# A two-layer hybrid decoder on one Trainium2 core: the first mixer's key selection placed later in the engines' order

## The chip, the cores and the metric

The kernel runs on one core of one Trainium2 chip. The metric is the device time of one execution in microseconds (us), lower is better. The engines are named as in the profile: PE is TensorE (matmuls), PEld its weight loads, DVE VectorE, ACT ScalarE, POOL GpSimd, SP the sync engine, whose queue issues nearly all transfers. A row with a q (SPq) is an engine's own queue of transfers.

## The reference

Two decoder layers over 512 positions of width 1024, all in float32. Both layers are feed-forward, mixer, feed-forward; the first layer's mixer is the one that the change is about. Cut to what matters there:

```python
for layer in range(2):
    h = h + 0.5 * swiglu(rmsnorm(h, g[0]), ...)      # 1024 -> 2816 -> 1024
    h = h + (hybrid_ab_mixer if layer == 0 else swa_sink_mixer)(rmsnorm(h, g[1]), ...)
    h = h + 0.5 * swiglu(rmsnorm(h, g[2]), ...)

def hybrid_ab_mixer(u, table, w_in, cq_g, wq_b, wq_idx, w_out):
    qa, ka, va, cq, kb, vb, k_idx, w_idx = split(u @ w_in)
    o_a = dilated_mixture(qa, ka, va, table[:, :8])          # heads 0 to 7, no selection
    cq = rmsnorm(cq, cq_g)
    qb, q_idx = cq @ wq_b, cq @ wq_idx                       # q_idx: 8 index heads of 32
    # selection: score[t, s] = scale * sum_h w_idx[t, h] * relu(q_idx[t, h] . k_idx[s]), s <= t
    # each position keeps its 128 best keys (topk = min(256, 512 // 4))
    o_b = dsa_attention(qb, kb, vb, q_idx, k_idx, w_idx, table[:, 8:], 128)   # heads 8 to 15
    return concatenate([o_a, o_b]) @ w_out
```

Every head adds a relative-position bias, whose table (32 buckets by 16 heads) is shared by all. Only heads 8 to 15 of the first mixer read the selection.

## The kernel before, in words

Activations lie transposed in SBUF, eight tiles of 128 features by 512 positions. Products are made in three matmuls on operands that are split into a high part (a cast) and a low part (a subtraction): high by low, low by high, high by high. These are L366 to L368 for the projections, L581 to L583 in the feed-forward, L748 and L749 for a head's logits. So each weight that comes in (L328, 512 KB) is cast on ScalarE (L336) and subtracted from by the helper `sub` (L315), on VectorE or, where the call allows it, on GpSimd. Keys and queries of a head pair are split the same way (casts L372, copies L693/L696, low parts L315).

**Who sets the order.** The kernel first describes every operation (`Plan.op`): the engines that may run it, a model duration, what it reads and writes, and a number `v`, its place in a nominal TensorE time `vt` that grows by each matmul's model duration. Then `Plan.emit` makes the order, one operation at a time: of each engine's candidates whose inputs are planned it takes the one that its model lets start first, and among those within 20 ns the one of smallest `v`. Buffers are slots of fixed pools (58 of 128x512 called s2, 20 weight tiles called d4, 8 PSUM banks), with limits per kind (`LIMIT`, `RESERVE`); `slot_time` answers whether and when an operation's buffers are to be had. An engine then runs its instructions in exactly that order, so an instruction that waits holds up all behind it, on SP's queue too.

**The first mixer** (`hybrid`). First come two products for the low-rank query, the index keys `kst` and the eight query stacks `qst`, each put together by three transfers from SBUF to SBUF (L891, 24 in all, on SP). Then `project(0)` makes value, key and query of the first two heads. `select` lists the selection: 24 scores, for three blocks of 128 queries times eight index heads, each a matmul (L932, 256, 384 or 512 columns) into a PSUM bank of which it may have four, a relu on ScalarE (L935) and a weighted sum on VectorE (L939, L942 for the first of a block, L946 for the others); then 16 rounds of MAX8 (L954) and MATCH_REPLACE8 (L956) for each block on VectorE, each taking the eight largest out; then three masks (L962). It gives these steps values `v` spread evenly between two numbers. After it come, for j from 0 to 7, `attend(j)` (two heads) and `project(j + 1)`; only j of 4 and more reads the masks.

**The bias tables.** GpSimd's queue writes the 16 tables of the first mixer (`tab0`) and those of the last (`tab1`) to memory in the first part of the run. Each head loads its own (L661, by SP) into an s2 slot of the kind `toep`, of which there may be five at a time; a load's `v` is 8000 below the nominal time at which it is described.

The constants are `SELECT_NS = 135000` and those quoted with the change. Line numbers are those of the profile before; in the changed kernel the same lines stand 2 to 7 further down (L366 is L373, L336 is L343, L315 is L322, L328 is L335, L372 is L379, L661 is L668, L748 is L755, L932 is L939, L935 is L942).

Of the kernel before, what the change touches and what calls it, by code (L numbers as in the profile page):

```python
# [35 lines left out]

LIMIT = {'mm': 4, 'sc': 2, 'sci': 4, 'pt': 2, 'ptv': 1, 'o': 6, 'tmp': 6, 'relu': 2, 'score': 3, 'qx': 6, 'toep': 5, 'prob': 6, 'turn': 3, 'sq': 2, 'q': 4, 'k': 4, 'vf': 3, 'of': 4, 'gt': 16, 'wraw': 6, 'cq2': 2, 'xn': 10, 'sa': 2, 'sb': 2, 'sk': 2}
RESERVE = {'q': 8, 'vf': 4, 'whl': 3, 'wraw': 5}


class Buf:
# [74 lines left out]
class Plan:  # L116
# [55 lines left out]
    def emit(self, make):  # L172

        for o in self.ops:
            o.deps.discard(o)
            o.left = len(o.deps)
            for d in o.deps:
                d.nexts.append(o)
            for b in o.bufs:
                b.left = b.users  # L180
        now = {}
        cand = {}
        blocked = set()
        free = {t: [0.0] * n for t, n in CAPACITY.items()}
        held, turn = {}, {}

        def offer(o):
            for i, (e, _, _) in enumerate(o.alts):
                cand.setdefault(e, {})[o.index] = o
                now.setdefault(e, 0.0)  # L190

        def slot_time(o):
            t, need = 0.0, {}
            for b in o.alloc:
                if held.get(b.kind, 0) + need.get(b.kind, 0) >= LIMIT.get(b.kind, 1 << 30):
                    return None
                if b.rank != turn.get(b.kind, 0) + need.get(b.kind, 0):
                    return None
                need[b.kind] = need.get(b.kind, 0) + 1
                n = need[b.tag, 0] = need.get((b.tag, 0), 0) + 1  # L200
                f = free[b.tag]
                if len(f) < n + RESERVE.get(b.kind, 0):
                    return None
                t = max(t, f[n - 1])
            return t

        for o in self.ops:
            if o.left == 0:
                offer(o)
        count, total = 0, len(self.ops)  # L210
        while count < total:
            best = None
            for e, cs in cand.items():
                s_e, items = None, []
                for o in cs.values():
                    st = max(now[e], o.ready)
                    if o.alloc:
                        t = slot_time(o)
                        if t is None:
                            continue  # L220
                        st = max(st, t)
                    if len(o.alts) > 1:
                        mine = next(ns for x, ns, _ in o.alts if x == e)
                        if any(max(now[x], st) + ns < st + mine - 1.0 for x, ns, _ in o.alts if x != e):
                            continue
                    items.append((st, o))
                    if s_e is None or st < s_e:
                        s_e = st
                if s_e is None:
                    continue  # L230
                if best is None or s_e < best[0]:
                    o = min((x for x in items if x[0] <= s_e + 20.0), key=lambda x: (x[1].v, x[1].index))
                    best = (s_e, o[0], e, o[1])
            if best is None:
                raise RuntimeError("schedule is stuck: " + str([
                    (e, sorted((o.v, [(b.kind, b.rank) for b in o.alloc]) for o in cs.values())[:3]) for e, cs in cand.items()]) + str(held) + str(turn))
            _, st, e, o = best
            for x, _, _ in o.alts:
                cand[x].pop(o.index, None)
            i = [a[0] for a in o.alts].index(e)  # L240
            _, ns, fn = o.alts[i]
            for b in o.alloc:
                f = free[b.tag]
                f.sort()
                f.pop(0)
                held[b.kind] = held.get(b.kind, 0) + 1
                turn[b.kind] = turn.get(b.kind, 0) + 1
                b.t = make(b)
            fn()
            now[e] = st + ns  # L250
            o.fin, o.eng, o.done = st + ns + o.lat, e, True
            for b in o.bufs:
                b.fin = max(b.fin, o.fin)
                b.left -= 1
                if b.left == 0:
                    free[b.tag].append(b.fin + self.HOP)
                    free[b.tag].sort()
                    held[b.kind] -= 1
            for n in o.nexts:
                n.ready = max(n.ready, o.fin + (self.SAME.get(e, 0.0) if all(a[0] == e for a in n.alts) else self.HOP))  # L260
                n.left -= 1
                if n.left == 0:
                    offer(n)
            count += 1
        self.end = max(now.values())


class Trunk:
# [578 lines left out]
    def hybrid(self, nxt):  # L847
# [138 lines left out]
        o = []  # L986
        project(0, True)
        T, T_next = [self.toeplitz(self.tab0, h, S) for h in range(2)], list(range(2, 16))
        v0 = self.vt - 12000
        select(v0, v0 + SELECT_NS)  # L990
        for j in range(8):
            attend(j)
            if j < 7:
# [240 lines left out]
SELECT_NS = 135000.0  # L1234
# [87 lines left out]
```

## Time and profile before

| | before |
|---|---|
| median of 3 runs | 1855.19 us (1854.97 to 1855.77) |
| the profiled execution | 1856.36 us, its span 1854.6 us |
| PE busy | 1811.5 us, 98% |
| DVE busy | 1398.2 us, 75% |
| ACT busy | 936.2 us, 50% |
| POOL busy | 245.1 us, 13% |

The span is the stretch from the first to the last instruction of the profiled execution. Busy shares are averages over all stages; the first mixer takes about 395 to 760 us of the span. Times of rows are counted from the span's start. A "releaser" in brackets behind a row is what ended the idle time of its engine.

### The profile page before, as it was taken

The numbers are of one execution on the slowest core, as the hardware profiler recorded it, in microseconds if no ns is written. First come the engines' busy times: TensorE is split into PE (matmuls) and PEld (weight loads), VectorE is DVE, ScalarE is ACT, GpSimd is POOL, SyncE is SP. The second block draws the span as 40 slices with busy tenths as digits, with TensorE's granted clock in tenths as the row PEclk, the third lists the DMA queues.
The fourth block names the chain that finished last, engine by engine and source line by source line (L and its number), as shares of the span: only waits on it lengthen the run. The fifth ranks groups of instructions, "written<-read, shape, count | busy, mean of one in ns | idle before, by whom it ended". The sixth has DMA issues, their size and how long they took to land.

```text
span 1854.6 us, 28373 instructions
## 1 busy us (share of the span) xinstructions
PE 1811.5 (98%) x11174; PEld 1619.7 (87%) x11178; DVE 1398.2 (75%) x2222; ACT 936.2 (50%) x1558; POOL 245.1 (13%) x240
## 2 busy tenths in 40 slices
PE   8899999989999999999999999999999999999997
PEld 6789989867877789899998989989888889899896
DVE  7965866759998898487588965857789898567483
ACT  6443533636757746254264543525569655345153
POOL 1500001024622120010001000001023120010010
PEclk9899999999999999999999999999999999999999
DMA  6463233432222323234334223323412223243131
GB/s 210 121 207 101 84 101 106 126 103 77 87 59 78 93 71 121 62 108 132 91 103 125 69 91 103 125 70 103 137 60 69 86 80 95 78 124 126 60 112 46
DMA packets 65431, 185.45 MB, mean 100 GB/s; under 512 B 11985, under 2 KB 14769, under 8 KB 65297
## 3 DMA queue, kind: packets, MB, share of 16 engines
q1 hardware_dynamic: 58176, 176.88, 30.9%
q0 software_dynamic: 6688, 6.66, 1.3%
q8 instruction: 87, 1.43, 0.3%
q14 instruction: 48, 0.39, 0.1%
q10 hardware_dynamic: 432, 0.10, 0.0%
HBM read 179.81 MB, written 8.47 MB: 102 GB/s over the span
## 4 chain that ended last, share of the span: by engine, by line
PE 81%; DVE 12%; issue 2%; ACT 2%; DMA 2%; POOL 1%; SPq 1%; DVEq 0%; POOLq 0%; ACTq 0%
PE ps L581 12%; PE ps L582 12%; PE ps L583 12%; PE ps L366 11%; PE ps L367 11%; PE ps L368 11%; DVE d L315 3%; DVE s L315 2%; PE ps L837 1%; DMA d<-in_w 1%; PE ps L839 1%; PE ps L838 1%; PE ps L797 1%; DVE s L755 1%; DVE s L471 1%
## 5 line engine op out<-in xcount | busy, mean ns | idle before, releaser
L336 ACT CAST d<-d 128x1024 fp32r<-128x1024 f32 (+4 forms) x492 | 448.6, 927 | 405.0 <-DMA d<-in_w 223.3
L315 DVE TENSOR_TENSOR d<-d,d 128x1024 fp32r<-128x1024 f32 (+3 forms) x475 | 507.1, 1084 | 176.1 <-ACT d L336 155.0
L581 PE MATMUL ps<-s,d 128*128 128x256 f32 x2016 | 572.2, 284 | 10.9 <-DVE d L315 7.9
L582 PE MATMUL ps<-s,d 128*128 128x256 f32 x2016 | 571.5, 283 | 0.0
L583 PE MATMUL ps<-s,d 128*128 128x256 f32 x2016 | 571.4, 283 | 0.0
L366 PE MATMUL ps<-s,d 128*128 128x512 f32 x1188 | 471.8, 397 | 3.6 <-DVE d L315 3.6
L367 PE MATMUL ps<-s,d 128*128 128x512 f32 x1188 | 465.1, 392 | 0.2
L368 PE MATMUL ps<-s,d 128*128 128x512 f32 x1188 | 464.7, 391 | 0.0
L581 PEld LDWEIGHTS ps<-s,d 128*128 128x128 f32 x2016 | 388.0, 192 | 12.5 <-DVE d L315 8.2
L582 PEld LDWEIGHTS ps<-s,d 128*128 128x128 f32 x2016 | 388.0, 192 | 0.5
L583 PEld LDWEIGHTS ps<-s,d 128*128 128x128 f32 x2016 | 387.9, 192 | 0.0
L366 PEld LDWEIGHTS ps<-s,d 128*128 128x128 f32 x1188 | 224.4, 189 | 47.9 <-DVE d L315 3.8
L368 PEld LDWEIGHTS ps<-s,d 128*128 128x128 f32 x1188 | 224.0, 189 | 47.8
L367 PEld LDWEIGHTS ps<-s,d 128*128 128x128 f32 x1188 | 224.5, 189 | 42.9 <-DVE s L315 0.5
L594 ACT COPY d<-ps 128x512 f32<-128x512 f32 x144 | 84.4, 586 | 217.6 <-PE ps L583 217.5
L653 DVE SCALAR_TENSOR_TENSOR s<-ps,s 128x512 f32<-128x512 f32 x88 | 60.7, 690 | 137.0 <-PE ps L368 136.8
L315 DVE TENSOR_TENSOR s<-s,s 128x512 fp32r<-128x512 f32 (+2 forms) x188 | 148.7, 803 | 7.3 <-ACT s L372 2.1
L533 POOL TENSOR_TENSOR d<-d 128x512 f32<-128x512 f32 x18 | 23.6, 1313 | 937.1 <-DVE d L533 807.1
L597 DVE TENSOR_TENSOR d<-ps,d 128x512 f32<-128x512 f32 x108 | 73.5, 686 | 32.7 <-PE ps L583 32.1
L533 DVE TENSOR_TENSOR d<-d,d 128x512 f32<-128x512 f32 x133 | 87.5, 686 | 1.7
L533 DVE TENSOR_TENSOR d<-d 128x512 f32<-128x512 f32 x126 | 85.6, 695 | 2.2
L764 ACT ACTIVATE s<-s,stat 128x256 f32<-128x256 f32 (+3 forms) x128 | 65.9, 516 | 24.6 <-DVE stat L755 23.9
(147 smaller groups left out, 1872.0 us busy)
## 6 DMA issues: line engine op xcount, KB each, us to landing
d<-in_w SPq DMA_DIRECT2D x234, 512.0 KB, 3.7
d<-in_w SPq DMA_DIRECT2D x32, 384.0 KB, 3.2
d<-in_hyb_in SPq DMA_DIRECT2D x22, 512.0 KB, 3.9
d<-in_swa_in SPq DMA_DIRECT2D x10, 512.0 KB, 3.6
tab<-rv POOLq DMA_DIRECT2D x4, 1024.0 KB, 16.7
s<-tab SPq DMA_DIRECT2D x16, 256.0 KB, 4.0
d<-in_hyb_out SPq DMA_DIRECT2D x16, 256.0 KB, 2.9
d<-in_swa_out SPq DMA_DIRECT2D x16, 256.0 KB, 2.7
```

The lines of the kernel that those rows point to most:

```text
L315: return lambda: eng.tensor_sub(out(), a(), b().bitcast(F32))
L336: alts = [("act", ns[0](n), lambda: nc.scalar.copy(hl.at(0, o), raw.t[:, c]))]
L366: nc.tensor.matmul(o, wl, xh.t, start=i == 0, stop=False)
L367: nc.tensor.matmul(o, wh, xl.t, start=False, stop=False)
L368: nc.tensor.matmul(o, wh, xh.t, start=False, stop=i == n - 1)
L533: return lambda: eng.tensor_add(o.t[:, oc], a.t[:, ac], o.t[:, oc])
L581: nc.tensor.matmul(o, wl, xh, start=start and m == 0 and k == 0, stop=False, skip_group_check=True)
L582: nc.tensor.matmul(o, wh, xl, start=False, stop=False, skip_group_check=True)
L583: nc.tensor.matmul(o, wh, xh, start=False, stop=k == 3, skip_group_check=True)
L594: self.act(sca_ns(S) - 40, lambda: nc.scalar.copy(view(q, c), bank(ps)), [ps], [(q, key)])
L597: self.dve(vec_ns(S), lambda: nc.vector.tensor_add(view(q, c), bank(ps), view(q, c)), [ps, (q, key)], [(q, key)])
L764: nc.scalar.activation(x, x, AF.Exp, bias=st.t[:, qb:qb + 1], scale=-1.0, accum_out=st.t[:, 4 + qb:5 + qb])
```

## The change

Two things. A new dict `AHEAD` and a running number `front` in `Plan.emit`: an operation that takes a buffer of the kind `toep` is no candidate as long as its `v` lies more than 30000 above the largest `v` of a TensorE operation placed so far. And in `hybrid` the selection's values `v` begin 12000 later, at the nominal time behind `project(0)`, and end 6000 later.

```diff
+AHEAD = {'toep': 30000.0}
...
     def emit(self, make):
...
+        front = -1.0e9
...
         def slot_time(o):
             t, need = 0.0, {}
             for b in o.alloc:
+                if b.kind in AHEAD and o.v > front + AHEAD[b.kind]:
+                    return None
...
             fn()
+            if e == "pe":
+                front = max(front, o.v)
...
         T, T_next = [self.toeplitz(self.tab0, h, S) for h in range(2)], list(range(2, 16))
-        v0 = self.vt - 12000
-        select(v0, v0 + SELECT_NS)
+        v0 = self.vt
+        select(v0, v0 + SELECT_NS - 6000)
```

The instructions are the same in kind and number; 15 of VectorE's subtractions become GpSimd's. TensorE's order is the same up to its row 2374, where the first mixer begins.

On SP, in the first feed-forward, this stands in the order before (`s` from `tab` is a bias table's load, `d` from `in_w` a feed-forward weight's):

```order
L328 DMA d_692<-in_w 128x1024
L661 DMA s_858<-tab_69 128x512
L328 DMA d_875<-in_w 128x1024
L661 DMA s_893<-tab_69 128x512
L661 DMA s_908<-tab_69 128x512
L661 DMA s_911<-tab_69 128x512
L328 DMA d_927<-in_w 128x1024
L661 DMA s_946<-tab_69 128x512
L328 DMA d_952<-in_w 128x1024
```

and this in the changed kernel:

```order
L335 DMA d_692<-in_w 128x1024
L335 DMA d_872<-in_w 128x1024
L335 DMA d_919<-in_w 128x1024
L335 DMA d_940<-in_w 128x1024
L335 DMA d_960<-in_w 128x1024
L335 DMA d_1100<-in_w 128x1024
L335 DMA d_1116<-in_w 128x1024
```

The five table loads are gone from among the weights. In the changed kernel the first of them stands ahead of the first mixer.

On TensorE, where the first mixer's group projections (L366 to L368, in the changed kernel L373 to L375) meet the first scores (L932, now L939), before:

```order
L368 MATMUL ps<-s_3643,d_3534 128x512
L932 MATMUL ps<-s_3794,s_3808 128x256
L932 MATMUL ps<-s_3794,s_3817 128x256
L366 MATMUL ps<-s_3432,d_3567 128x512
L367 MATMUL ps<-s_3440,d_3538 128x512
L368 MATMUL ps<-s_3432,d_3538 128x512
L366 MATMUL ps<-s_3442,d_3567 128x512
L367 MATMUL ps<-s_3452,d_3538 128x512
L368 MATMUL ps<-s_3442,d_3538 128x512
L712 MATMUL ps<-ident,s_3909 128x128 x4
L932 MATMUL ps<-s_3794,s_3821 128x256
```

and now:

```order
L373 MATMUL ps<-s_3637,d_3592 128x512
L374 MATMUL ps<-s_3647,d_3590 128x512
L375 MATMUL ps<-s_3637,d_3590 128x512
L939 MATMUL ps<-s_3792,s_3806 128x256
L939 MATMUL ps<-s_3792,s_3815 128x256
L939 MATMUL ps<-s_3792,s_3819 128x256
L939 MATMUL ps<-s_3792,s_3825 128x256
L939 MATMUL ps<-s_3792,s_3829 128x256
L373 MATMUL ps<-s_3422,d_3627 128x512
L374 MATMUL ps<-s_3430,d_3594 128x512
L375 MATMUL ps<-s_3422,d_3594 128x512
L939 MATMUL ps<-s_3792,s_3850 128x256
```

The rows of before are the end of the value's projection (its weight is `d_3534`) and the start of the key's (`d_3567`, `d_3538`), with scores in between; in the changed kernel no score stands within the key's and the query's projections: the rows are the end of the query's (`d_3592`), then five scores in a row, then the next head pair's value (`d_3627`). A little further, the first head's logits, before (L748, L749):

```order
L366 MATMUL ps<-s_3482,d_3633 128x512
L367 MATMUL ps<-s_3489,d_3604 128x512
L368 MATMUL ps<-s_3482,d_3604 128x512
L748 MATMUL ps<-d_4009,s_4090 128x128
L749 MATMUL ps<-d_4009,s_4090 128x128
```

and now (L755, L756), with two scores directly ahead of them:

```order
L373 MATMUL ps<-s_3472,d_3627 128x512
L374 MATMUL ps<-s_3479,d_3594 128x512
L375 MATMUL ps<-s_3472,d_3594 128x512
L939 MATMUL ps<-s_3792,s_3905 128x256
L939 MATMUL ps<-s_3792,s_3910 128x256
L755 MATMUL ps<-d_3961,s_4015 128x128
L756 MATMUL ps<-d_3961,s_4015 128x128
```

Before, 20 scores stand ahead of these logits, now 8; the three groups of the next value's projection that stand ahead (its weight's high part is `d_3633`, now `d_3627`) are the same.

On ScalarE, casts of weights (L336, now L343), casts and copies of the first key (L372 and L693, now L379 and L700) and relus (L935, now L942), before:

```order
L935 ACTIVATE s_3913<-ps 128x256
L935 ACTIVATE s_3915<-ps 128x256
L723 CAST v<-ps 128x8x64
L935 ACTIVATE s_3940<-ps 128x256
L935 ACTIVATE s_3949<-ps 128x256
L935 ACTIVATE s_3959<-ps 128x256
L935 ACTIVATE s_3969<-ps 128x256
L336 CAST d_3971<-d_3924 128x1024
L935 ACTIVATE s_3992<-ps 128x256
L935 ACTIVATE s_4002<-ps 128x256
L935 ACTIVATE s_4004<-ps 128x384
L372 CAST d_4009<-s_3990 64x512
```

and now:

```order
L730 CAST v<-ps 128x8x64
L343 CAST d_3943<-d_3912 128x1024
L379 CAST d_3961<-s_3954 64x512
L379 CAST d_3966<-s_3954 64x512
L700 CAST d_3961<-s_3954 64x512
L700 CAST d_3966<-s_3954 64x512
L343 CAST d_3989<-d_3948 128x1024
L942 ACTIVATE s_4003<-ps 128x256
L942 ACTIVATE s_4011<-ps 128x256
L379 CAST s_4015<-s_3999 64x512
L379 CAST s_4024<-s_3999 64x512
L942 ACTIVATE s_4030<-ps 128x256
```

Seven relus stood ahead of the first weight's cast (128x1024) and of the key's casts (64x512); now two weights' casts and the key's casts and copies stand ahead of the first relu.

## Rows read from the trace of the kernel before

**Rows 1.** The page's first part: engine, busy us, share, instructions.
```profile
PE 1811.5 (98%) x11174; PEld 1619.7 (87%) x11178; DVE 1398.2 (75%) x2222; ACT 936.2 (50%) x1558; POOL 245.1 (13%) x240
```

**Rows 2.** Five stretches of the first mixer; columns in the second line.
```profile
core 0: us, PE busy (x) PEld busy (x) DVE busy (x) ACT busy (x) POOL busy (x), PEclk, DMA share, GB/s
410.00:420.00 10.00, 6.81 (x24) 5.33 (x23) 5.04 (x7) 4.69 (x9) 3.93 (x3) 0.83 0.52 137
420.00:430.00 10.00, 7.20 (x33) 5.76 (x31) 9.58 (x14) 5.61 (x12) 2.85 (x2) 0.96 0.27 79
430.00:440.00 10.00, 9.87 (x36) 8.42 (x37) 8.58 (x28) 8.84 (x24) 1.49 (x3) 0.70 0.38 134
440.00:560.00 120.00, 116.66 (x600) 96.47 (x600) 118.94 (x299) 73.55 (x161) 59.18 (x55) 1.00 0.23 69
560.00:640.00 80.00, 77.56 (x412) 63.19 (x414) 68.85 (x140) 58.22 (x129) 14.38 (x23) 1.00 0.29 88
```

**Rows 3.** SP's timeline: start, us, engine, line, operation, count.
```profile
395.56 13.78 SPq L891 DMA_DIRECT2D s<-s  x20
409.43 0.53 SPq L328 DMA_DIRECT2D d<-in_hyb_in  x1
410.00 2.41 SPq L891 DMA_DIRECT2D s<-s  x4
```

**Rows 4.** PE's timeline, the first mixer's scores and logits.
```profile
403.35 0.40 PE L932 MATMUL ps<-s,s 96*128 96x256 f32 x2
...
410.49 0.40 PE L366 MATMUL ps<-s,d 128*128 128x512 f32 x1
...
411.18 0.39 PE L366 MATMUL ps<-s,d 128*128 128x512 f32 x1
...
415.22 0.36 PE L932 MATMUL ps<-s,s 96*128 96x256 f32 x1 [3.19 <-DMA s<-s]
...
423.52 1.39 PE L932 MATMUL ps<-s,s 96*128 96x384 f32 x6
...
430.13 0.48 PE L748 MATMUL ps<-d,s 128*128 128x128 f32 x1 [2.93 <-DVE s L315]
...
461.05 0.33 PE L748 MATMUL ps<-d,s 128*128 128x128 f32 x1 [0.79 <-POOL s L315]
```

**Rows 5.** ACT's timeline, the same stretch.
```profile
414.52 1.04 ACT L336 CAST d<-d 128x1024 fp32r<-128x1024 f32 x1 [4.14 <-DMA d<-in_hyb_in]
...
417.78 1.24 ACT L372 CAST d<-s 64x512 fp32r<-64x512 f32 x2
419.05 0.49 ACT L935 ACTIVATE s<-ps 128x384 f32<-128x384 f32 x1
```

**Rows 6.** DVE's timeline, the same stretch.
```profile
412.06 0.69 DVE L685 TENSOR_TENSOR s<-ps,s 128x512 f32<-128x512 f32 x1 [1.17 <-PE ps L368]
...
420.53 2.10 DVE L315 TENSOR_TENSOR d<-s,d 64x512 fp32r<-64x512 f32 x3
...
423.59 3.92 DVE L946 SCALAR_TENSOR_TENSOR s<-s,wts,s 128x384 f32<-128x384 f32 x3
427.42 0.68 DVE L669 SCALAR_TENSOR_TENSOR s<-ps,s 128x512 f32<-128x512 f32 x1
...
429.38 1.41 DVE L315 TENSOR_TENSOR s<-s,s 64x512 fp32r<-64x512 f32 x2
```

**Rows 7.** POOL's timeline, the same stretch: subtractions for weights.
```profile
415.64 2.37 POOL L315 TENSOR_TENSOR d<-d,d 128x1024 fp32r<-128x1024 f32 x1 [19.72 <-PE ps L932]
...
423.25 2.40 POOL L315 TENSOR_TENSOR d<-d,d 128x1024 fp32r<-128x1024 f32 x1 [2.79 <-ACT d L336]
...
448.83 4.89 POOL L315 TENSOR_TENSOR d<-d,d 128x1024 fp32r<-128x1024 f32 x2 [5.28 <-ACT d L336]
```

**Rows 8.** SP's waits, 40 to 125 us: total, times, longest.
```profile
SPq L661 <- DMA tab<-rv: 24.1, 1, 24.1
```

**Rows 9.** SP's table loads (L661) by line: times, first and last start.
```profile
L661 SPq EVENT_SEMAPHORE  x16: 17/28/24082, 64.6 to 1397.9; - x16
```

**Rows 10.** PE's timeline in the first feed-forward.
```profile
99.73 0.39 PE L581 MATMUL ps<-s,d 128*128 128x256 f32 x1 [0.70 <-ACT d L594]
...
103.86 0.39 PE L581 MATMUL ps<-s,d 128*128 128x256 f32 x1 [1.01 <-ACT d L594]
```

**Rows 11.** ACT's timeline there.
```profile
101.77 1.05 ACT L336 CAST d<-d 128x1024 fp32r<-128x1024 f32 x1 [1.57 <-DMA d<-in_w]
```

**Rows 12.** DVE's search steps (L956) by line.
```profile
L956 DVE MATCH_REPLACE8 s<-m,s x48: 398/543/687, 423.3 to 551.8; 128x256 f32<-128x256 f32 x16, 128x384 f32<-128x384 f32 x16, 128x512 f32<-128x512 f32 x16
```

## The prediction

> **What bounds the kernel now.** I read the page's first part, then the stretches of the first mixer, then the timelines of the queues and engines in the one stretch that is not full, and last the place where the early table loads stand. TensorE is busy 98% of the span [rows 1], so only its idle time and its time at the lower clock can be won. The stretches show where those are: between 410 and 440 us TensorE idles 3.19 + 2.80 + 0.13 = 6.1 us, and the granted clock is 0.83, 0.96 and 0.70, that is, at the lower of its two levels (1.2 GHz instead of 2.4) for 3.4 + 0.8 + 6.0 = 10.2 us, which costs half of it, 5.1 us [rows 2]. From 440 to 560 VectorE is busy 118.94 of 120 us and TensorE 116.66: there both are nearly full and VectorE sets the pace. From 560 to 640 VectorE has 11.15 us idle [rows 2].
>
> The hole at 410 to 440 has two causes. The score matmuls (L932) need query stacks that 24 small transfers build; SP issues 20 of them from 395.56 to 409.34, then a weight load at 409.43, then the rest [rows 3]. TensorE reaches the seventh score before its stack has landed and waits 3.19 us, to 415.22, with the projections of the first group standing behind it in its order [rows 4]. Then the first head's logits wait 2.93 us, to 430.13, for the query's low part (L315) [rows 4]: the projection was done at 423.52, but VectorE stood in three score steps from 423.59 for 3.92 us, took the query at 427.42 and finished its low parts at 430.79 [rows 6].
>
> **The change part by part.** *The table loads.* At 64.6 us SP stops at the first of five table loads and waits 24.1 us for the table to be written, with the loads of the next weights behind it [rows 8, 9]. TensorE pays 0.70 + 1.01 us, when its release came from ScalarE [rows 10], which stood at a cast that waits for such a weight load [rows 11]. The order shows the five gone from there and that layer otherwise unmoved. I take -1.7; the bounds are 0, if the loads now wait for the table's own transfers or for buffers, and -2.5, if short waits behind it go as well. The stage after it is full, so the gain stays. In the mixer and in the last mixer the table loads come later but still ahead of the heads that read them; I take 0 for those (bounds 0 and +0.8, the last wait of rows 4 as the nearest).
>
> *The 24 scores on TensorE.* Before, 20 of them stand ahead of the first head's logits; now 8 do, all behind the 16 groups of three matmuls that project the first group's key and query. A group takes 0.69 [rows 4], so from 403.35 they end at 403.35 + 16 x 0.69 + 0.4 (transposes) = 414.8 without a wait. Four scores follow to 415.5; the fifth needs a PSUM bank that a ScalarE relu frees. In ScalarE's new order the cast of a later weight stands ahead of the key's casts and of the relus, and that weight is still issued at 409.43 [rows 3]: so ScalarE waits to 414.52 as before. Then: that cast to 415.56, two key casts of 0.62 to 416.8, two copies to 418.0, another cast of 1.04 to 419.1, first relu to 419.5 [rows 5]. So TensorE waits 415.5 to 419.5: the first wait is not removed, it goes from 3.19 to 4.0 and from the transfer to ScalarE.
>
> *The query's low parts.* VectorE needs the key casts (416.8) and, for three key subtractions, the end of the POOL split that starts at 415.6 and takes 2.40 [rows 7]: 418.0 + 3 x 0.70 = 420.1; query 0.68 to 420.8; two query casts to 422.1; low parts 1.41 to 423.5 [rows 5, 6]. If POOL's next split comes first, up to 2.4 more. I take 424.5. TensorE has the last four of the eight scores and three groups to do meanwhile, which at the lower clock fill 419.5 to about 424, so a second wait, and the second fall of the clock, should be gone. Against 430.13 this is 5.6 us earlier, but 12 scores are still to be done: six take 1.39 less the overlap [rows 4], 0.20 each, 2.4 in all. So TensorE is 3.2 us ahead, and the 6.0 us at the lower clock behind 430 [rows 2] give another 3.0: -6.2 at the second group's first logits, which is TensorE's row 2588 in both orders (461.05 before [rows 4]).
>
> *VectorE pays.* In ScalarE's wait it idles, where before it had scores to add up. At 424.5 it has 13 more score steps before it than before at 430.8 (by the orders; 0.62 for 384 columns, from the 3.92 of rows 6 less a stall of 2.06, and an estimated 0.48 for 256) and a pair of search steps, some 8.2 us: 424.5 + 8.2 = 432.7, 1.9 behind. POOL's splits of three later weights, of which two ran beside the search before (448.83 [rows 7]), now fall among score steps. A score step that met a split at 423.25 to 425.65 lost 2.06 us [rows 6, 7], so each costs between 0 and 2.4; half gives +3.6. Four fewer instructions of 512 columns on VectorE (by the order; an estimated 0.5 each against 0.70 for such a subtraction) give -2.0. So VectorE is 3.5 us late.
>
> The Trainium skill bears on this term: "SBUF — State Buffer", section "Who interferes with whom", says that a VectorE instruction with two SBUF inputs and a GpSimd one that reads SBUF share a port pair that the first holds to its end. By that rule the three splits cost VectorE from 0 to 7.2 us, as the issue falls; the stall in rows 6 agrees with it. The rule speaks against this change; the sum stands without it.
>
> *The sum in the mixer.* If VectorE's lateness is hidden in full, the mixer gains 6.2; if not at all, it loses 3.5. The selection now ends later, with later projections put ahead of the heads that need it, and VectorE has 11.15 us idle between 560 and 640 [rows 2] for the 9.7 between the ends; but the heads there have chains of their own. I take two thirds hidden: -6.2 + 3.2 = -3.0. With the table loads -4.7. The profiled execution took 1856.36 us (span 1854.6 and 1.8 around it), so 1851.7 by its own time; the median of the runs is 1.2 lower: 1850.5.
>
> **The rivals.** *VectorE takes it back.* Only a third is hidden: -6.2 + 6.5 = +0.3, and with the table loads -1.4: 1853.8. For it speaks VectorE's 99% from 440 to 560, against it the idle time behind 560.
>
> *The search ends too late.* Nothing is hidden, and a masked head of the second half waits on TensorE long enough for another fall of the clock, as at 430 (3.0): +3.5 + 3.0 - 1.7 = +4.8, 1860.0, slower. It decides where VectorE's last search step, at 551.8 before [rows 12], ends later than about 562. Against it: the new order has two more projections ahead of those heads.
>
> *The hole closes.* If ScalarE's wait is short and the splits fall kindly, all 6.1 + 5.1 us between 410 and 440 go, with the table loads -12.9: 1842.3. Against it stands the cast at 414.52, whose load is issued behind the same 20 transfers.
>
> That the change doesn't do what it says is excluded by the orders.
>
> **How the numbers follow.** Forecast 0.36 (its own range 1847 to 1852), VectorE takes it back 0.33, search too late 0.16, hole closes 0.15. What this kernel's measurement can tell from no change is 0.2%, 3.7 us. Faster: 0.15 and most of the forecast, 0.46; same: 0.33 and the forecast's upper end, 0.38; slower 0.16. The range 1842.5 to 1858.5 leaves out the far parts of the two outer cases.
>
> **What would show it.** No wait of SP for the table at 64 us, and the two TensorE waits of rows 10 gone. ScalarE's cast at about 414 still waiting for its load, TensorE waiting for a relu from about 415 to 419 instead of a transfer, and the first logits at 423.5 to 426 without a second wait of about 3 us. VectorE full to some 560 and its score steps stretched under POOL's splits. The prediction is wrong if that cast's load lands before 412, if the second wait stays, or if heads behind 560 make TensorE wait in all over 5 us.

## The result and the profile after: slower, not faster

The changed kernel takes 1867.54 us (median of 4 runs, 1864.73 to 1870.08), the kernel before 1855.08 beside it (4 runs, 1854.65 to 1855.77): a ratio of 1.0066 [1.0047, 1.0086], 12.5 us slower where 4.6 faster had been forecast, and outside the range. The profiled execution of the changed kernel is its fastest run: 1864.73 us with a span of 1862.5, against 1856.36 and 1854.6 before.

The first question is in which stage the time went. Every stage ends where TensorE transposes the statistics of the next norm (L430 before, L437 after), which gives a mark that needs no model. TensorE's timeline before, at the marks around the first mixer and the two feed-forwards behind it:

```profile
383.91 0.65 PE L430 MATMUL ps<-ident,tiny 128*128 128x128 f32 x4 [1.26 <-DVE tiny L414]
...
658.11 0.60 PE L430 MATMUL ps<-ident,tiny 128*128 128x128 f32 x4
...
1004.35 0.65 PE L430 MATMUL ps<-ident,tiny 128*128 128x128 f32 x4
...
1350.74 0.60 PE L430 MATMUL ps<-ident,tiny 128*128 128x128 f32 x4
```

And after:

```profile
383.57 0.65 PE L437 MATMUL ps<-ident,tiny 128*128 128x128 f32 x4 [1.27 <-DVE tiny L421]
...
661.28 0.60 PE L437 MATMUL ps<-ident,tiny 128*128 128x128 f32 x4
...
1009.53 0.60 PE L437 MATMUL ps<-ident,tiny 128*128 128x128 f32 x4
...
1358.66 0.60 PE L437 MATMUL ps<-ident,tiny 128*128 128x128 f32 x4
```

The same marks of all stages, as differences, in us:

| | first feed-forward | first mixer | second feed-forward | third feed-forward | last mixer | last feed-forward |
|---|---|---|---|---|---|---|
| before | 350.99 | 274.20 | 346.24 | 346.39 | 148.93 | 345.70 |
| after | 351.74 | 277.71 | 348.25 | 349.13 | 148.95 | 345.69 |
| difference | +0.75 | +3.5 | +2.0 | +2.7 | 0.0 | 0.0 |

One thing moves across a mark. TensorE's matmuls of one projection line between the marks of the second feed-forward (count | busy us, mean ns of one | idle before), before:

```profile
L366 PE MATMUL ps<-s,d 128*128 128x512 f32 x240 | 93.6, 390 | 0.0
```

and after:

```profile
L373 PE MATMUL ps<-s,d 128*128 128x512 f32 x241 | 94.0, 390 | 0.0
```

A group of three matmuls, 0.7 us, is done behind the mixer's mark now and was done ahead of it before. By the work done, the mixer therefore loses 4.2 us and the second feed-forward 1.3.

The first stage begins 1.1 us earlier, so the stages' 9.0 us leave 7.9 in the span. 4.1 of the 9.0 lie where the prediction had not looked at all: in the second and third feed-forward, whose code the diff does not touch.

In the mixer the stretches that answer to [rows 2], columns as there:

```profile
410.00:420.00 10.00, 7.35 (x36) 5.83 (x34) 5.74 (x3) 5.03 (x8) 6.10 (x3) 1.00 0.48 157
420.00:430.00 10.00, 7.13 (x26) 6.16 (x27) 8.47 (x25) 7.18 (x19) 0.79 (x2) 0.66 0.40 132
430.00:440.00 10.00, 9.02 (x54) 7.70 (x53) 9.47 (x20) 9.93 (x23) 5.69 (x7) 1.00 0.10 29
440.00:560.00 120.00, 112.21 (x553) 92.84 (x553) 118.12 (x281) 69.48 (x151) 55.70 (x51) 0.99 0.24 73
```

The hole between 410 and 440 is not smaller: TensorE idles 2.65 + 2.87 + 0.98 = 6.5 us instead of 6.1. The granted clock is down in one stretch only: 6.8 us at the lower level (0.66) instead of 10.2. And from 440 to 560, where TensorE had been busy 116.66 us, it is busy 112.21. Summed over windows of 10 us from mark to mark, TensorE idles 17.3 us in the mixer instead of 12.8, and its time at the lower clock is 10.2 us in both: the mixer's loss is waiting. TensorE's timeline after, waits and first rows of interest:

```profile
115.27 0.49 PE L373 MATMUL ps<-s,d 128*128 128x512 f32 x1 [1.81 <-ACT s L630]
...
421.90 0.80 PE L939 MATMUL ps<-s,s 96*128 96x256 f32 x2 [4.55 <-DVE s L676]
423.67 0.47 PE L755 MATMUL ps<-d,s 128*128 128x128 f32 x1 [0.97 <-DVE s L322]
...
462.51 0.47 PE L755 MATMUL ps<-d,s 128*128 128x128 f32 x1 [4.24 <-POOL s L322]
...
704.89 0.38 PE L588 MATMUL ps<-s,d 128*128 128x256 f32 x1 [1.19 <-ACT d L601]
...
1053.73 0.38 PE L588 MATMUL ps<-s,d 128*128 128x256 f32 x1 [2.46 <-ACT d L601]
```

The first logits start at 423.67, 6.5 us earlier than before; the second group's start at 462.51, 1.5 us later [rows 4]. What was won up to 424 is lost by 462, and 1.5 us more: over half of it in the one wait of 4.24 us, the rest in two waits of 0.98 and 0.92 us at 440 and 443 and in the twelve scores that were still to be done. The last two rows are new waits in the two feed-forwards. VectorE's timeline after, in between:

```profile
414.21 6.91 DVE L322 TENSOR_TENSOR d<-s,d 64x512 fp32r<-64x512 f32 x3 [4.38 <-ACT d L379]
421.15 0.69 DVE L676 SCALAR_TENSOR_TENSOR s<-ps,s 128x512 f32<-128x512 f32 x1
...
436.86 2.19 DVE L953 SCALAR_TENSOR_TENSOR s<-s,wts,s 128x384 f32<-128x384 f32 x1
...
439.57 3.03 DVE L953 SCALAR_TENSOR_TENSOR s<-s,wts,s 128x384 f32<-128x384 f32 x2
...
446.86 0.62 DVE L953 SCALAR_TENSOR_TENSOR s<-s,wts,s 128x384 f32<-128x384 f32 x1
447.39 2.63 DVE L830 CAST s<-s 128x512 fp32r<-128x512 f32 x1
...
453.84 0.74 DVE L953 SCALAR_TENSOR_TENSOR s<-s,wts,s 128x512 f32<-128x512 f32 x1
454.83 1.45 DVE L953 SCALAR_TENSOR_TENSOR s<-s,wts,s 128x512 f32<-128x512 f32 x1
...
457.90 0.55 DVE L961 MAX8 m<-s 128x8 f32<-128x384 f32 x1
...
459.58 0.68 DVE L676 SCALAR_TENSOR_TENSOR s<-ps,s 128x512 f32<-128x512 f32 x1
```

And GpSimd's, the same stretch:

```profile
413.74 2.40 POOL L322 TENSOR_TENSOR d<-d,d 128x1024 fp32r<-128x1024 f32 x1 [18.18 <-ACT d L343]
416.22 1.61 POOL L322 TENSOR_TENSOR d<-s,d 64x512 fp32r<-64x512 f32 x1
417.90 2.67 POOL L322 TENSOR_TENSOR d<-d,d 128x1024 fp32r<-128x1024 f32 x1
...
436.24 2.39 POOL L322 TENSOR_TENSOR d<-d,d 128x1024 fp32r<-128x1024 f32 x1 [2.55 <-ACT d L343]
439.08 2.38 POOL L322 TENSOR_TENSOR d<-d,d 128x1024 fp32r<-128x1024 f32 x1 [0.45 <-DVE s L953]
447.12 2.61 POOL L322 TENSOR_TENSOR d<-d,d 128x1024 fp32r<-128x1024 f32 x1 [5.66 <-ACT d L343]
...
453.93 6.85 POOL L322 TENSOR_TENSOR d<-s,d 64x512 fp32r<-64x512 f32 x4
461.04 2.77 POOL L322 TENSOR_TENSOR s<-s,s 64x512 fp32r<-64x512 f32 x2 [0.27 <-ACT s L379]
```

The two are to be read side by side. Each VectorE subtraction or score step that reads both its tensors from SBUF and starts within a GpSimd subtraction is stretched: three subtractions take 6.91 us where they took 2.10 [rows 6]; the score step at 436.86 takes 2.19 and the one at 446.86, beside nothing, 0.62; the cast at 447.39 takes 2.63; 512-column steps go from 0.74 at 453.84 to 1.45 at 454.83. The MAX8 at 457.90, in the same company, takes 0.55 and is not touched, and neither is L676 at 459.58 (0.68), which reads one tensor from PSUM. Before, from 448.83 on [rows 7], mostly MAX8 and MATCH_REPLACE8 stood beside GpSimd's work.

### The profile page after: what moved, and what is told of

Same layout as the page of the kernel before. It is cut to its first block, busy times and chain, and to the rows that moved or that the text cites. A ratio compares the mean times of both kernels' runs of the same rounds, so it can differ in the third digit from the quotient of the medians.

```text
span 1862.5 us, 28407 instructions
## 1 busy us (share of the span) xinstructions
PE 1810.3 (97%) x11178; PEld 1619.2 (87%) x11178; DVE 1402.3 (75%) x2207; ACT 934.9 (50%) x1558; POOL 269.7 (14%) x255
## 4 chain that ended last, share of the span: by engine, by line
PE 81%; DVE 12%; ACT 3%; issue 2%; DMA 1%; POOL 1%; SPq 0%; DVEq 0%; ACTq 0%; POOLq 0%
PE ps L588 13%; PE ps L589 13%; PE ps L590 13%; PE ps L373 11%; PE ps L374 11%; PE ps L375 11%; DVE d L322 3%; DVE s L322 2%; PE ps L844 1%; PE ps L846 1%; PE ps L845 1%; DVE s L478 1%; DMA d<-in_w 1%; DVE s L762 1%; PE ps L804 1%
## 5 line engine op out<-in xcount | busy, mean ns | idle before, releaser
L343 ACT CAST d<-d 128x1024 fp32r<-128x1024 f32 (+4 forms) x492 | 447.9, 927 | 391.0 <-DMA d<-in_w 225.1
L588 PE MATMUL ps<-s,d 128*128 128x256 f32 x2016 | 572.1, 284 | 12.8 <-DVE d L322 7.9
L373 PE MATMUL ps<-s,d 128*128 128x512 f32 x1188 | 470.1, 396 | 5.4 <-DVE d L322 3.6
L375 PE MATMUL ps<-s,d 128*128 128x512 f32 x1188 | 464.2, 391 | 0.0
L373 PEld LDWEIGHTS ps<-s,d 128*128 128x128 f32 x1188 | 224.0, 189 | 50.6 <-DVE d L322 3.2
L375 PEld LDWEIGHTS ps<-s,d 128*128 128x128 f32 x1188 | 223.5, 188 | 47.9
L540 POOL TENSOR_TENSOR d<-d 128x512 f32<-128x512 f32 x21 | 28.5, 1357 | 917.0 <-DVE d L540 538.7
L322 DVE TENSOR_TENSOR s<-s,s 128x512 fp32r<-128x512 f32 (+2 forms) x190 | 153.0, 818 | 5.6 <-ACT s L630 1.5
```

What stands on the lines that cost most here:

```text
L322: return lambda: eng.tensor_sub(out(), a(), b().bitcast(F32))
L343: alts = [("act", ns[0](n), lambda: nc.scalar.copy(hl.at(0, o), raw.t[:, c]))]
L373: nc.tensor.matmul(o, wl, xh.t, start=i == 0, stop=False)
L375: nc.tensor.matmul(o, wh, xh.t, start=False, stop=i == n - 1)
L540: return lambda: eng.tensor_add(o.t[:, oc], a.t[:, ac], o.t[:, oc])
L588: nc.tensor.matmul(o, wl, xh, start=start and m == 0 and k == 0, stop=False, skip_group_check=True)
```

## The experiments

The theory behind the runs: half of the loss is the collision just shown, inside the mixer; the other half is a new order of ScalarE in the second and third feed-forward, which the planner wrote because it had a different state when it came there. The rivals: that it is all mixer and the waits behind it cost nothing; that the later table loads cost, or gain, in the first feed-forward; that the time in the mixer is VectorE's sheer amount of work and not who stands beside whom; and, for small differences, mere spread between executions. Runs are compared by their ratio to the kernel before, timed beside them (its medians were 1855.1 to 1856.0).

To hold one part of the program still while another changes, some kernels make the order in two passes: a first one finds an order, a second one takes over from the first the order and engines of all operations described behind the first mixer, and plans the rest anew. In `plan(limits, old, pin)` the second argument chooses the old values of the selection, the third is the first pass's order; without a third it is the plain kernel's one pass.

**The changed kernel again**, unchanged.

> The changed kernel once more, for its second level: its first four runs lie at 1864.7, 1865.2, 1869.9 and 1870.1 us, with mean granted clocks of 0.991 to 0.992 and 0.988. Theory: the 5 us between them is one more fall of TensorE's clock in the first mixer (0.004 of 1867 us less mean clock is about 15 us at half clock, 5 to 7 us of time), behind the wait of 4.24 us at 462.5 or the one of 4.55 at 421.9; a profile at the upper level shows a stretch of clock near 0.5 to 0.7 there that the first profile does not have. Rival: the 5 us are longer waits for transfers in the feed-forward layers, with the clock as before there.

Measured: 1866.56 us (1864.68 to 1869.5), 1.0063 [1.0051, 1.0076]; stages 351.40, 278.02, 348.25, 349.08. The loss and its places repeat. The profiled run is one of the shorter ones (1866.03), so the expectation's question, where the runs near 1870 lose their 5 us more, is not decided.

**The limit alone**: `AHEAD` stays, the selection's values go back.

```diff
-        v0 = self.vt
-        select(v0, v0 + SELECT_NS - 6000)
+        v0 = self.vt - 12000
+        select(v0, v0 + SELECT_NS)
```

> Only the new limit on table loads; the selection keeps its old values. TensorE's order is that of the kernel before up to row 3275 (near the end of the first mixer); ScalarE's, VectorE's and GpSimd's orders in the second feed-forward are nearly those of the changed kernel. Theory (three losses: mixer +4.2, second feed-forward's order +3.7, first feed-forward +0.8, read by comparing the two traces at the same instructions): 1855.1 + 3.7 + 0.8 = 1859.6, 1858.5 to 1860.5. Rival, the selection's place is the whole loss: 1855 +- 1. By the prediction's term for the table loads: 1855.1 - 1.7 = 1853.4.

Measured: 1861.57 (1858.18 to 1863.71), 1.0032 [1.0019, 1.0045]; mixer 271.37, feed-forwards behind it 348.24 and 350.52. So the limit is enough to spoil the two later feed-forwards, and the mixer's part comes from the shift of the selection. The shift without the limit was not run, since it has no order: the planner comes to a point where no operation can be placed. Tables of the last mixer hold all five of their slots there.

**The new mixer with the old rest**: everything described behind the first mixer is held to the order and engines that the kernel before has.

```diff
-        seq = self.plan(AHEAD, False)
+        seq = self.plan(AHEAD, False, self.plan({}, True))
```

> The changed kernel, with everything behind the first mixer held in the order and on the engines that it has in the kernel before (two planning passes; the second one follows the first for all operations described behind the mixer). Theory: the waits of 1.19 us at 704.9 and 2.46 us at 1053.7 go, 1864.7 - 3.7 = 1861, or 1866 where the second level shows. Rival: these waits come from where the weight loads stand in time, not from ScalarE's order, and stay: 1864.7 or 1870.

Measured: 1861.72 (1860.24 to 1864.15), 1.0036 [1.0024, 1.0049]; mixer 279.14, then 346.14 and 346.15, as before. **The old mixer with the new rest** is its complement:

```diff
-        seq = self.plan({}, True)
+        seq = self.plan({}, True, self.plan(AHEAD, False))
```

> The kernel before, with everything behind the first mixer held in the order of the changed kernel; against the kernel with the limit alone it differs only in SP's five table loads in the first feed-forward. Theory: 1855.1 + 3.7 = 1858.8, and the limit alone is 0 to 1 us slower than this, because the time that the table wait gave back is taken by a later wait for a weight. By the prediction's term (the table wait is worth 1.7 us) the limit alone is 1.7 us faster than this. Rival, the rest's order costs nothing: 1855 +- 1.

Measured: 1862.36 (1861.89 to 1862.52), 1.0039 [1.0025, 1.0052]; mixer 272.98, then 348.26 and 350.47. The two parts, +6.5 and +7.0 us by the means against the runs of before beside them, add up to 13.5; the whole change has +11.5 on that chip. So the halves are about equal, and independent to within 2 us. That the rest costs nothing is refuted by both runs.

**Two copies first.** ScalarE's timeline of the changed kernel shows what TensorE waits for in the third feed-forward at 1053.73:

```profile
1051.22 1.98 ACT L343 CAST d<-d 128x1024 fp32r<-128x1024 f32 x2
1053.10 0.57 ACT L601 COPY d<-ps 128x512 f32<-128x512 f32 x1
```

The copy reads the PSUM bank that TensorE's next product needs, and it stands behind two casts of weights. At 702.38 two casts stand ahead of a copy in the same way. This kernel is the changed one with these two copies moved ahead of the two casts and the activation before them; all other instructions of all engines keep their order.

```diff
+        for k in (2653, 3645):
...
+            seq.remove((k - 1, "pe"))
+            seq.remove((k, "act"))
+            i = seq.index((k - 2, "pe"))
+            seq[i + 1:i + 1] = [(k - 1, "pe"), (k, "act")]
```

> The changed kernel with two of ScalarE's instructions moved, nothing else: in the second and the third feed-forward the copy (L601) for which TensorE waits 1.19 and 2.46 us goes ahead of the two weight casts and the activation that stand directly before it. Theory: it is this place in ScalarE's order that costs, not the order of VectorE or GpSimd there nor the transfers: both waits fall under 0.3 us, the two stages come down from 348.2 to 346.7 and from 349.1 (or 350.5 with a fall of the clock) to 346.5, and the time from 1866.6 to 1862 (1860.5 to 1863.5). Rival, the stage is late as a whole and the copy only shows it: the wait moves to another instruction behind it and the stages stay at 348.2 and 349.1 or more: 1865 to 1868.

The changed kernel ran beside it:

> The changed kernel on the same chip, to be compared with e11: 1866.6 (1864.7 to 1870 as in the earlier runs), stages of the second and third feed-forward 348.2 and 349.1, or 350.5 where the clock falls behind the wait of 2.46 us.

Measured: 1862.97 (1860.5 to 1865.2), 1.0042 [1.0029, 1.0054], against 1866.7 (1865.27 to 1867.65), 1.0063 [1.0049, 1.0077]; the means differ by 3.6 us. ScalarE's timeline with the copy moved:

```profile
1053.87 0.58 ACT L633 COPY d<-ps 128x512 f32<-128x512 f32 x1
...
1054.87 2.00 ACT L375 CAST d<-d 128x1024 fp32r<-128x1024 f32 x2
```

Both of TensorE's waits are gone, and the stages are 347.27 and 346.80 instead of 348.25 and 349.19. Two instructions of 0.57 us, put too late in the order, carry 3.4 of the 4.8 us between these marks. Of the other 1.4 us, 0.7 is the group of matmuls that moved across the mark; the rest is not explained, since TensorE idles 0.1 us at most in these two stages and its clock is full.

**Two subtractions to VectorE.** The third kernel again, with the two GpSimd subtractions of weights that stand beside the key's subtractions (413.74 and 417.90 above) done by VectorE at the same place of the order. If the collision is the cost, this gains, though VectorE gets more work (1.22 us each); if the amount of work is, it loses. In the edit `o.tag[1]` issues the same subtraction on VectorE.

```diff
+TAKE = (6, 8)
...
+            if e == "pool" and o.tag:
+                took += 1
+                if took - 1 in TAKE:
+                    o.tag[1]()
+                    continue
```

> The kernel of e3 (changed mixer, old order behind it; 1861.7 us), with two subtractions for weights, GpSimd's at 413.7 and 417.9 us, done by VectorE in the same place of the plan. Theory, contention: VectorE's three key subtractions, which took 6.91 us beside GpSimd's instead of 2.10, take 2.1 again; VectorE does 2.4 us more, so the query's product is 2.4 to 2.5 us earlier, the first logits come 2.5 us earlier (425.0 to 422.5) and so do the second ones (463.4 to 461): 1859.2 (1857.5 to 1860.5). Rival, load: VectorE has too much to do before the second logits, however it is shared, and 2.4 us more on it makes that wait longer: 1861.7 to 1864.

Measured: 1859.84 (1857.03 to 1861.02), 1.0016 [1.0007, 1.0025]; mixer 276.98. **Five of them** (`TAKE = (6, 8, 9, 10, 11)`, with the three at 436.24, 439.08 and 447.12):

> As e5, with GpSimd's next three subtractions for weights too (436.2, 439.1, 447.1 us), beside which score steps and a cast on VectorE lost 1.6, 1.8 and 1.4 us. Theory, contention: VectorE does 3 x 1.22 = 3.7 us more and loses 4.8 less: 1.1 better than e5, about 1858 (1856.5 to 1859.5). Rival, load: 3.7 worse than e5.

Measured: 1856.65 (1854.21 to 1859.57), 1.0005 [0.9996, 1.0014], 2.6 ± 1.4 us less than the one with two, beside which it ran; mixer 272.94. VectorE's timeline with five:

```profile
415.15 1.22 DVE L355 TENSOR_TENSOR d<-d,d 128x1024 fp32r<-128x1024 f32 x1 [4.03 <-ACT d L378]
416.29 3.10 DVE L355 TENSOR_TENSOR d<-s,d 64x512 fp32r<-64x512 f32 x3
...
438.21 1.33 DVE L988 SCALAR_TENSOR_TENSOR s<-s,wts,s 128x384 f32<-128x384 f32 x2
...
445.47 0.42 DVE L865 CAST s<-s 128x512 fp32r<-128x512 f32 x1
```

The three subtractions take 3.10 instead of 6.91, the pair of score steps 1.33 instead of 3.03, the cast 0.42 instead of 2.63. More work on VectorE, and the mixer is 6 us shorter than with the five on GpSimd (the third kernel): the collision is the cost. It is paid in two ways: from mark to mark TensorE idles 13.6 us instead of 17.3, and it spends 3.4 us at the lower clock instead of 13.8. That GpSimd was simply short of time is excluded by its own timeline after: it idled 3.16 us, until VectorE's L692 was done, before it began on the second pair's key at 452.89. What is left is a mixer as long as the old one, so no run shows a gain of the later selection itself. With two alone only part is its doing: the second group's logits move 0.8 us, and the rest of that mixer's 2.2 is a shorter fall of the clock at 460 to 470 (granted 0.83 instead of 0.66).

**Eleven of them.** The one below (five, early tables) with six subtractions of the second pair's keys and queries moved too (`TAKE` with 12 to 17 more).

> As e8, with GpSimd's six subtractions for the second pair's keys and query (450.9 to 460.8 us in e6) done by VectorE too. Contention: five score steps of 512 columns there take 1.15 to 1.45 us /1 instead of 0.74, about 2.7 us lost in all, and the query's two take 2.8 us on GpSimd and 1.4 on VectorE; against it stand 6 x 0.70 = 4.2 us of work for VectorE. The two nearly balance: e8 -0.5 (-2 to +1.5).

Measured: 1859.59 (1858.12 to 1861.03), 1.002 [1.0011, 1.0029], 1.5 ± 1.2 us more than the same kernel without the six. The wait ahead of the second group's logits is 4.37 us, and VectorE itself is what ends it. Here the rival wins. The six did hit something: beside them four score steps took 1.15 to 1.45 us, and without them 0.74 to 0.75, which is 2.3 us won. But they take VectorE 4.7 us, and VectorE sets the pace.

**The table loads.** The kernel before with the limit for the last mixer's tables alone, the feed-forwards behind the mixer held to the old order (`mark2` is the number of the last mixer's first operation):

```diff
-                if b.kind in AHEAD and o.v > front + AHEAD[b.kind]:
+                if b.kind in ahead and o.index >= self.mark2 and o.v > front + ahead[b.kind]:
```

> The kernel before with the limit for the last mixer's tables alone, and the second and third feed-forward held in their old order. In e2 and e4 the first mixer took 271.4 and 273.0 us against 274.2 before, and its only change of order stands near its end, where the last mixer's tables no longer take slots. Theory: the old feed-forward costs nothing more, the mixer's end gives 1.2: 1854.7 against 1855.9 for before. Rival: those 1.2 us are spread of the clock between executions: 1855.9 +- 0.6.

Measured: 1856.12 (1853.53 to 1858.31), 1.0002 [0.9993, 1.0011]: not told apart from the kernel before. And the kernel with five on VectorE, with the first mixer's five table loads back in the first feed-forward:

> The kernel of e6 (1856.65 us) with the limit for the last mixer's tables alone, so that SP's five table loads stand in the first feed-forward again, as before; every other engine's order is that of e6. Theory: SP's wait there costs TensorE nothing that a later wait for a weight does not take anyway, and without it TensorE waits 2.2 to 2.6 us at once near 116 us and loses clock behind that: 0.6 to 1.7 us better than e6, 1855.5 (1854.5 to 1856.3). By the prediction's term for the table wait: 1.7 worse, 1858.4.

Measured: 1858.19 (1855.01 to 1860.68), 1.0011 [1.0002, 1.0019], 1.3 ± 1.6 us above the kernel without them, from another chip. It leans to the prediction's side, but no stage shows it: the first feed-forward took 351.98 us on average in the six profiled kernels with early loads and 352.25 in the eight with late ones.

**The old mixer with two subtractions on VectorE**: the kernel with the last mixer's tables late, and `TAKE = (6, 8)`, there the GpSimd work at 415.6 and 423.25 [rows 7].

> The kernel of e7 (old selection, 1856.1 us) with GpSimd's subtractions for weights at 415.6 and 423.3 us done by VectorE. Theory, contention also bounds the kernel before: the score step that lost 2.06 us beside the second one loses nothing, against 1.22 us of work, so the wait of 2.93 us before the first logits shrinks by 0.8, and the clock may fall for less long: 1855.2 (1853.5 to 1856.2). Rival, load: 1.2 to 2.4 worse, 1857.5 to 1858.5.

Measured: 1854.87 (1852.99 to 1856.16), 0.9994 [0.9985, 1.0003]. The hole that the change was aimed at gets smaller by itself, as TensorE's timeline shows:

```profile
429.87 0.33 PE L790 MATMUL ps<-d,s 128*128 128x128 f32 x1 [1.09 <-DVE s L355]
```

The wait had been 2.93 [rows 4]. It has the lowest median of all, but it is not told apart from the kernel before. By the ratios it lies 1.5 us below the kernel with the tables late alone, which is within the spread; if it is real, part of the collision's price is older than the change.

## Why the prediction was wrong

Three steps failed. Everything behind the mixer was counted as unmoved and lost 4.1 us. The mixer's gain hung on "-6.2 at the second group's first logits", where +1.5 was measured. And the 1.7 us of the table loads did not stay.

*SP's wait for the table and the waits of [rows 10]: right, and worth nothing.* SP no longer stops at 64 us, and both waits are gone. In their place come 1.81 + 0.36 + 0.57 us at 115 to 120. ScalarE's timeline after shows a cast there that waits 7.48 us for its weight, where the longest such wait between 90 and 125 us had been 4.33:

```profile
110.48 1.05 ACT L343 CAST d<-d 128x1024 fp32r<-128x1024 f32 x1 [7.48 <-DMA d<-in_w]
```

The step that failed is "The stage after it is full, so the gain stays": SP's loads now wait for weight buffers, that is, for the engine that reads one last, and the gain of 1.7 was handed back 15 us later. SP's longest waits of this kind from 40 to 125 us, after (total, times, longest):

```profile
SPq L335 <- DVE d L322: 29.4, 5, 13.0
SPq L335 <- PE ps L590: 24.1, 5, 10.7
```

All its waits that VectorE or TensorE ended sum to 77.6 us there, and to 51.7 before: more than the 24.1 us of the table's wait came back. The term was at its end of 0, for the reason that the prediction had given for that end ("or for buffers").

*The first wait: right in size, wrong in its place and cause.* Predicted 4.0 us ahead of the fifth score, measured 4.55 ahead of the seventh, to 421.90. The prediction let the fifth score wait for a PSUM bank that a relu of ScalarE frees, and ScalarE for its cast at 414.5. But six scores ran from 414.38 to 415.96, before the first relu began at 417.25, and the cast came at 412.62, after its load, a little over the 412 at which the prediction called itself wrong. What ended TensorE's wait was VectorE's L676, which reads the projected query out of PSUM at 421.15, behind the 6.91 us of subtractions. The prediction named this ("if POOL's next split comes first, up to 2.4 more") with 2.4 as its most; it was 4.8.

*The first logits and the second wait: right, the time in part by luck.* 424.5 predicted, 423.67 measured; the second wait 0.97 instead of 2.93. Two errors cancelled: VectorE began the key's subtractions at 414.21, where the sum had 418.0, and took 6.91 us for them, where the sum had 2.10.

*"-6.2 at the second group's first logits": wrong, +1.5.* This is the step in the mixer that failed. The prediction added up TensorE's own lead here and held VectorE's lateness apart from this point ("3.5 us late", to be hidden later), but these very logits need VectorE's query and then GpSimd's low parts of it. On VectorE's timeline before:

```profile
458.30 0.69 DVE L669 SCALAR_TENSOR_TENSOR s<-ps,s 128x512 f32<-128x512 f32 x1
```

and on GpSimd's:

```profile
459.72 2.63 POOL L315 TENSOR_TENSOR s<-s,s 64x512 fp32r<-64x512 f32 x2 [0.18 <-ACT s L372]
```

After, the two stand at 459.58 and 461.04, each 1.3 us later, and the logits come 1.5 us later. TensorE's own wait there had been 0.79 us [rows 4]: as long as the query came no sooner, TensorE could win no more than that, however early it was. The row was in the prediction's hands.

And the price of the collision was mis-sized: for the splits +3.6 had been taken, with bounds 0 and 7.2. VectorE's score steps from 395 to 462 us, grouped by shape (count | busy us, mean ns of one | idle before), before:

```profile
L946 DVE SCALAR_TENSOR_TENSOR s<-s,wts,s 128x384 f32<-128x384 f32 x7 | 6.2, 882 | 0.4
L946 DVE SCALAR_TENSOR_TENSOR s<-s,wts,s 128x512 f32<-128x512 f32 x7 | 5.4, 766 | 0.0
L946 DVE SCALAR_TENSOR_TENSOR s<-s,wts,s 128x256 f32<-128x256 f32 x7 | 5.3, 760 | 5.6 <-ACT s L935 5.4
```

and after:

```profile
L953 DVE SCALAR_TENSOR_TENSOR s<-s,wts,s 128x384 f32<-128x384 f32 x7 | 7.5, 1078 | 0.2
L953 DVE SCALAR_TENSOR_TENSOR s<-s,wts,s 128x512 f32<-128x512 f32 x7 | 7.5, 1068 | 0.0
L953 DVE SCALAR_TENSOR_TENSOR s<-s,wts,s 128x256 f32<-128x256 f32 x7 | 3.4, 488 | 0.3
```

The steps of 256 columns have lost their company and gain 1.9 us; those of 384 and 512 lose 1.3 and 2.1, the cast 1.4 (it took 1.23 us before), the key's subtractions 4.8; two smaller groups (L949, three of them, and one subtraction of 128x512) gain 1.4. That is net 6.3, 1.7 times the term and near its upper end; the term had counted three splits of weights and not GpSimd's parts of keys and queries. By the last search step VectorE is 12.7 us late (564.5 instead of 551.8), where 3.5 had been taken; the collision is part of that, and the rest was not followed.

The Trainium skill, "SBUF — State Buffer", section "Who interferes with whom", says that a VectorE instruction with at most one SBUF input, outside its two-port modes, does not contend with GpSimd, and one with two does, when GpSimd reads SBUF. The trace agrees on both: MAX8 0.55 us in the same company, score steps up to three and a half times their length. The cast has one input and is stretched too, so it would have to be in such a mode; no view here shows an instruction's mode.

*The rivals.* "VectorE takes it back" had the right mechanism and too small a size: the mixer lost 4.2 in the pair of profiles, where +0.3 had been given. Over more executions it is more: with the group that moved counted to the mixer in all of them, 278.8 on average with the new selection (five profiles), 272.9 with the old (before and three of the experiments), +5.9. "The search ends too late" had the right sign by another road. The last search step did come late, 564.5 instead of 551.8 and past the 562 at which that rival should decide, yet TensorE's waits on heads from 560 to 640 sum to under 3 us; it is not what cost the time. "The hole closes" did not come about: from 410 to 440 TensorE idles 6.5 us.

*The view that was missing.* 4.1 of the 9.0 us in the stages are lost behind the mixer. The prediction read the orders in the mixer and the first feed-forward alone and let everything behind count as unmoved. That two casts stand ahead of a copy there was in the new order, without a run. No term and no rival had it.

What stays open: the median of these four runs lies 2.8 us above the profiled one. Over all 14 runs of the changed kernel the time follows TensorE's mean granted clock, from 1864.7 us at 0.992 to 1870.1 at 0.988. A mean lower by 0.004 is some 15 us more at the lower level, an estimated 7 us at most, so the clock can account for the spread; in which stage it falls is not known, since no run above 1866.1 was profiled.

## What to carry to other kernels

When an order is made by a planner, a change of values in one stage can re-decide all stages behind it: compare every engine's order to the end of the program, and look there for a copy out of PSUM that has moved behind other work. Moving work on one engine also changes who it stands beside on another; price a step by its neighbour in the new order, and carry the price to the next instruction that needs both engines. An engine's lead counts only up to the wait that it has left at the next point where it meets another: read there who came last before, and by how much. A queue's long wait was worth nothing here, because the loads behind it then waited for buffers.

## What the runs showed of the hardware

A wait of the same length, at the same instruction, costs TensorE's clock in one kernel and not in another. The wait at the third feed-forward's copy was 2.46 us in the changed kernel and 2.48 in the one with the old mixer and the new rest; the stretch 1050 to 1060 of the changed kernel:

```profile
1050.00:1060.00 10.00, 7.54 (x63) 7.34 (x62) 7.27 (x9) 5.11 (x8) 0.00 (x0) 1.00 0.18 54
```

and of the other:

```profile
1050.00:1060.00 10.00, 9.61 (x67) 9.61 (x68) 4.82 (x7) 2.65 (x5) 0.00 (x0) 0.83 0.06 25
```

The granted clock is 1.00 in one and 0.83 in the other: 3.4 us at 1.2 GHz, a loss of up to 1.7. The stages are 349.1 and 350.5. It went the same way in each execution that was profiled: in three of the changed kernel the clock stayed up (waits of 2.46 to 2.48 us), and in both kernels with the old mixer and this wait it fell (2.47 and 2.48). Why is not shown. So a short wait has two prices here, its own length and sometimes 1 to 2 us more.

In the collision GpSimd loses little: 1.61 instead of 1.35 us for a 64x512 subtraction, 2.67 instead of 2.40 for a 128x1024 one, while VectorE's three took 6.91 instead of 2.10.
